# Input load order, modulation rows and HGRN head halves in a hybrid HGRN2 / mLSTM / PEER layer

## The chip, the cores and the metric

The kernel runs on one core of one Trainium2 chip. The metric is the device time of one execution in microseconds (us). A program that runs on the chip is compared by the median of several runs.

## The reference, cut to what matters

The layer takes 1024 latent tokens and 256 context tokens of width 1024. A conditioning vector gives six modulation vectors for the latent tokens and six for the context. Of these, the first two (shift and scale) are needed before anything else, the other four only behind the mixers.

```
mod_l = silu(c) @ w_mod + b_mod ; mod_c = silu(c_ctx) @ w_mod + b_mod
sh1, sc1, g1, sh2, sc2, g2 = split(mod, 6)            # for latent and for context tokens
p = (LN(tokens) * (1 + sc1) + sh1) @ w_in             # 9 blocks of 512 columns and 16 gate columns
o_hg = HGRN2 heads (4), forward and backward: S_t = diag(f_t) S_{t-1} + k_t v_t^T, o_t = S_t^T q_t,
       f = lb + (1 - lb) * sigmoid(z), k = 1 - f
h_ml = mLSTM heads (4), both directions, gates log_i = g_i, log_f = log_sigmoid(g_f)
x = LN(alpha * x + g1 * (readout @ w_out)) ; x = LN(alpha * x + g2 * PEER(LN(x) * (1 + sc2) + sh2))
```

PEER is a retrieval of 16 of 16384 single-neuron experts in each of 8 heads. It takes about two thirds of the time and is not touched.

## The kernel before, in words

Tokens lie in 10 tiles of 128: two of context, eight of x. Their modulated, transposed form xmT is kept as an f16 part and a bf16 remainder, so each projection is three matmul passes for each of 8 slices of the width.

**Prologue.** modcols (L84) loads two context tiles, then the first 2048 columns of w_mod in 8 row slices of 1 MB, and after half of these the weight block W(HI). Each slice feeds three matmuls of 2 x 512 (L116); the last 512 columns are done on VectorE as multiply-adds into macc (L120, L122). The eight x tiles are loaded after that. The sums are copied out (L126), and turned into columns by 16 matmuls with a ones vector and 12 transposes (L130, L132), which gives modc. inputs_ln (L164) takes the tiles in groups of 2, 4 and 4: statistics (L145, L147), normalisation (L170), transposes on TensorE (L176), scale and shift on ScalarE (L180), a cast to f16 on VectorE (L181), and the remainder on VectorE, or on GpSimd for every third slice (L182).

**Gates.** hgrn (L342) first calls gates (L237): 16 gate columns are projected for all tiles (into the bank oa), transposed to rows (L261), put through log-sigmoid as rows of 1280 (L266 to L270), scanned (L280 to L299), exponentiated, and transposed back into columns (L331), with a last small matmul group (L337). Then come modrows (L669), the values' projection inputs(0) and inputs(1) with 8 preparations of U behind each (uprep, L188), and the heads.

**modrows** computes the other four modulation vectors for the latent tokens: 32 tiles wm of 128 x 1024 in two buffers, for each of them two matmuls of 1 x 512 in quarters of the array, eight rows added to b_mod (L692) and stored to mrow (L693). mrow is read for g1 (L777) and for the mixing rows (L771), behind the mixers.

**Heads.** For each pair hh of heads the query weights are loaded and two heads projected (L500); then, for both directions d and both heads, one (L388) projects the forget gate (L222), takes sigmoid, logarithm and a scan (L394 to L404), builds the scaled keys and queries (L409 to L425), transposes keys (L431), and runs states, scores and outputs (L444 to L491). In it ten preparations of U are called: load of a 0.5 MB tile us (L195), cast on ScalarE (L198), remainder on GpSimd (L199), store (L202).

**Order.** The program is scheduled when it is built: each engine takes, by a modelled time line, what is ready and was written first; storage is given out in pools, and a tile that lies on an older tile's place waits for its readers. On the chip each engine then keeps that order. An instruction marked keep_in_program_order stays behind all that was written before it on its engine. All transfers here are issued by SP.

Of the kernel before, what the change touches and what calls it, by code (L numbers as in the profile page):

```python
# [6 lines left out]
F32 = mybir.dt.float32  # L7
# [81 lines left out]
def modcols(g, I, mp, lp):  # L89
# [16 lines left out]
    ps = [g.pp.tile([128, 512], F32, name=n, bufs=2 if n == "pj" else 1) for n in ("pj", "pj", "sc")]  # L106
# [17 lines left out]
    mr = mp.tile([128, 2048], F32, name="w0", bufs=8)[0:2]  # L124
    for b in range(3):
        (nc.scalar.copy if b % 2 else nc.vector.tensor_copy)(mr[:, b * 512:(b + 1) * 512], ps[b][0:2])  # L126
    pt = g.pp.tile([128, 512], F32, name="tr", bufs=2)
    for b in range(12, 16):
        for j in range(2):
            nc.tensor.matmul(pt[:, 2 * b + j:2 * b + j + 1], acc[:, j, (b - 12) * 128:(b - 11) * 128], g.ones, start=True, stop=True)  # L130
    for b in range(12):
        nc.tensor.transpose(pt[:, 2 * b:2 * b + 2], mr[:, b * 128:(b + 1) * 128], g.ident[0:2, 0:2])  # L132
    nc.vector.tensor_tensor(g.modc, pt[:, 0:32].rearrange("p (b j) -> p b j", j=2),
                            bT[:, :, None].to_broadcast([128, 16, 2]), op=OP.add)
# [29 lines left out]
def inputs_ln(g, xs, sp):  # L164

    nc = g.nc
    for t0, n in ((0, 2), (2, 4), (6, 4)):
# [4 lines left out]
        for k in range(KD):  # L172
# [8 lines left out]
            nc.vector.tensor_copy(g.xmT[0][:, k, sl], f)  # L181
# [55 lines left out]
def gates(g, I, w):  # L237
    nc, tc = g.nc, g.tc
    gp = g.gp
    with tc.tile_pool(name="gt", bufs=1, reuse_waits="tile") as tp:  # L240
        gb = tp.tile([128, 16], F32, name="gb")
# [1146 lines left out]
```

## Time and profile before

| what | value |
|---|---|
| median of 3 runs | 3186.1 us (3183.93 to 3199.63) |
| the profiled execution | 3201.39 us |
| its span | 3199.5 us, mean granted TensorE clock 0.952 |
| busy, share of the span | TensorE 91%, VectorE 80%, GpSimd 57%, ScalarE 37% |
| DMA | 900.31 MB, mean 281 GB/s |

The profile is of one execution, and its times count from the start of the span. The shares are averages over stages with different limits, so they say little about a change in the first 550 us: what such a change is worth is read from the stretches in which it acts and from what ends the waits there.

### The profile page before, as it was taken

To read this page: it belongs to the slowest core of one execution; us is meant where nothing else is said; L and a number is where in the kernel's file an instruction comes from. 1 tells how busy PE (TensorE), PEld (TensorE's weight loads), DVE (VectorE), ACT (ScalarE), POOL (GpSimd) and SP (SyncE) were. 2 spreads that over 40 slices of the span, in tenths; PEclk is the share of its full clock that TensorE was granted. 3 is DMA by queue.
4 is the path that set the end of the run, shared out by engine and by line. 5 is a ranking of instruction groups with operands and counts; after the bars stand their busy time and mean duration, and the time that the engine had idled before them with its cause. 6 is when DMAs were issued, how large, how long until landed. Compare 5 with 4: busy or idle time off the path is not lost.

```text
span 3199.5 us, 50493 instructions
## 1 busy us (share of the span) xinstructions
PE 2925.7 (91%) x18943; PEld 1890.1 (59%) x18943; DVE 2562.6 (80%) x5352; ACT 1180.8 (37%) x1699; POOL 1838.3 (57%) x1358
## 2 busy tenths in 40 slices
PE   7898999887898799899999999999999999999992
PEld 4644556556786566577778875555555555555541
DVE  8434464999878899798777777988888888888898
ACT  4464563325345432126666653222222222212211
POOL 3555675422347456416656666766666666666664
PEclk8999998998999899999999999999999999999996
DMA  7688666411267689767889999999999999999985
GB/s 282 212 290 290 214 207 238 145 60 60 100 214 268 225 297 333 276 232 261 294 283 312 316 345 338 371 347 350 364 363 362 363 341 368 362 357 364 358 306 190
DMA packets 319546, 900.31 MB, mean 281 GB/s; under 512 B 28077, under 2 KB 107573, under 8 KB 311365
## 3 DMA queue, kind: packets, MB, share of 16 engines
q1 hardware_dynamic: 208708, 494.38, 44.3%
q0 software_dynamic: 110592, 402.70, 33.6%
q8 instruction: 149, 2.44, 0.3%
q14 instruction: 97, 0.79, 0.1%
HBM read 758.67 MB, written 138.30 MB: 280 GB/s over the span
## 4 chain that ended last, share of the span: by engine, by line
PE 43%; DVE 26%; DMA 11%; issue 8%; POOL 6%; ACT 4%; SPq 0%; another core or an unknown queue 0%; DVEq 0%; POOLq 0%; ACTq 0%
PE y L1164 17%; PE S L1131 14%; DMA row<-in_peer_v_dram,idx 5%; DVE mz L555 3%; DVE row L1091 3%; PE pj L222 3%; PE y L1039 2%; DMA us<-in_peer_ut_dram 2%; DVE hg L1099 2%; POOL row L1072 2%; POOL uT L199 2%; PE pj L230 2%; DVE us L1034 1%; PE pj L833 1%; PE S L910 1%
## 5 line engine op out<-in xcount | busy, mean ns | idle before, releaser
L1131 PE MATMUL S<-hTd,uT 128*128 128x320 f16 (+1 forms) x6144 | 889.6, 301 | 15.6 <-ACT ge L1136 11.2
L1164 PE MATMUL y<-vs,w 128*128 128x512 bf16 x3840 | 857.3, 381 | 14.0 <-ACT vs L1146 6.8
L1131 PEld LDWEIGHTS <-uT 128*128 128x128 bf16 x6144 | 605.4, 99 | 270.8 <-issue 18.3
L1164 PEld LDWEIGHTS <-w 128*128 128x128 bf16 x3840 | 377.0, 98 | 452.3 <-issue 23.4
L1099 DVE SCALAR_TENSOR_TENSOR hg<-row,dot,hg 128x1024 f32<-128x1024 f32 x381 | 489.7, 1285 | 117.2 <-DMA row<-in_peer_v_dram,idx 107.8
L1072 POOL DMA_INDIRECT row<-in_peer_u_dram,idx x384 | 382.7, 997 | 288.2 <-DVE row L1091 144.6
L1072 POOL DMA_INDIRECT row<-in_peer_v_dram,idx x384 | 381.4, 993 | 215.2 <-DVE hg L1099 135.2
L1091 DVE SCALAR_TENSOR_TENSOR row<-row,hg 128x1024 f32<-128x1024 f32 x384 | 460.7, 1213 | 51.5 <-DMA row<-in_peer_u_dram,idx 48.5
L199 POOL TENSOR_TENSOR uT<-us,uT 128x1024 bf16<-128x1024 f32 x128 | 303.8, 2379 | 192.6 <-ACT uT L198 175.6
L1146 ACT CAST vs<-vf 128x1024 bf16<-128x1024 f32 x128 | 129.8, 1042 | 489.1 <-PE y L1164 255.4
L1147 POOL TENSOR_TENSOR vs<-vf,vs 128x1024 bf16<-128x1024 f32 x128 | 280.3, 2201 | 40.6 <-ACT vs L1146 37.4
L1035 POOL TENSOR_TENSOR kT<-us,gf 128x512 f32<-128x512 bf16 x160 | 177.3, 1135 | 193.8 <-DVE us L1034 158.1
L1136 ACT ACTIVATE ge<-S 128x320 f32<-128x320 f32 x256 | 112.6, 441 | 471.5 <-PE S L1131 377.7
L222 PE MATMUL pj<-xmT,wb 128*128 128x512 f16 (+3 forms) x1248 | 262.9, 367 | 19.3 <-ACT pad L545 17.6
L230 PE MATMUL pj<-wb,xmT 128*128 128x256 f16 (+1 forms) x1728 | 222.9, 289 | 25.2 <-DVE rsg L748 14.7
L1171 DVE TENSOR_TENSOR ya<-ya,y 128x512 f32<-128x512 f32 x310 | 210.1, 681 | 31.1 <-PE y L1164 29.6
L230 PEld LDWEIGHTS <-xmT 128*128 128x128 f16 (+1 forms) x1968 | 185.6, 103 | 67.6 <-issue 27.0
L222 PEld LDWEIGHTS <-wb 128*128 128x128 f16 (+1 forms) x1248 | 123.9, 101 | 147.4 <-issue 43.5
L1040 ACT COPY gst<-y 128x512 f32<-128x512 f32 x160 | 171.2, 1075 | 89.4 <-PE y L1039 69.6
L1034 DVE TENSOR_TENSOR us<-iob,eT 128x512 bf16<-128x512 bf16 x320 | 163.5, 559 | 25.5 <-ACT kT L1036 21.1
L198 ACT CAST uT<-us 128x1024 bf16<-128x1024 f32 x128 | 133.3, 1044 | 122.3 <-DMA us<-in_peer_ut_dram 101.5
L1039 PE MATMUL y<-kT 128*128 128x128 f32 x1280 | 161.5, 279 | 10.8 <-ACT kT L1036 9.8
(390 smaller groups left out, 3882.0 us busy)
## 6 DMA issues: line engine op xcount, KB each, us to landing
us<-in_peer_ut_dram SPq DMA_DIRECT2D x128, 512.0 KB
Ud<-uT SPq DMA_DIRECT2D x128, 512.0 KB
uT<-Ud SPq DMA_DIRECT2D x128, 512.0 KB
vf<-in_peer_v_dram SPq DMA_DIRECT2D x128, 512.0 KB
Gd<-gst SPq DMA_DIRECT2D x20, 1984.0 KB
Gt<-Gd SPq DMA_DIRECT2D x31, 1280.0 KB
Sd<-ge SPq DMA_DIRECT2D x66, 320.0 KB
kT<-Sd SPq DMA_DIRECT2D x66, 320.0 KB
```

Of the source, the lines that this page charges most:

```text
L199: nc.gpsimd.tensor_tensor(lo, uf, hi, op=OP.subtract)
L222: g.nc.tensor.matmul(ps[:, :t1 - t0], w.t[a][:, k, c0:c0 + 128], g.xmT[b][:, k, t0:t1], start=(k == 0 and a == b), stop=(k == KD - 1 and a ...
L230: g.nc.tensor.matmul(ps, g.xmT[a][:, k, t * 128:(t + 1) * 128], w.t[b][:, k, :w.n], start=(k == 0 and a == b), stop=(k == KD - 1 and a == 1))
L1034: nc.vector.tensor_tensor(cm[:, a], g.iob, eT[:, a, None, t0:t0 + 4].to_broadcast([128, 128, 4]), op=OP.is_equal)
L1039: nc.tensor.matmul(ps[:, i * 128:(i + 1) * 128], oh[:, 0, i], oh[:, 1, i], start=True, stop=True)
L1072: d = g.nc.gpsimd.indirect_dma_start(out=b, out_offset=None, in_=self.I["peer_u" if n < 128 else "peer_v"][0], in_offset=bass.IndirectOffs ...
L1091: nc.vector.scalar_tensor_tensor(b, b, 1.0, self.ps, op0=OP.mult, op1=OP.mult, accum_out=dot[:, j:j + 1])
L1099: nc.vector.scalar_tensor_tensor(self.ps, b, dot[:, j:j + 1], self.ps, op0=OP.mult, op1=OP.add)
L1131: m = nc.tensor.matmul(ps[:, :hn], uT[:, a, k, :], g.hTd[b][:, k, i * hn:(i + 1) * hn], start=(k == 0 and (a, b) == (0, 0)), stop=(k == KD ...
L1147: nc.gpsimd.tensor_tensor(v[:, 1], vf, v[:, 0], op=OP.subtract)
L1164: nc.tensor.matmul(ps, w[:, a, t * 128:(t + 1) * 128], v[:, b, h * 512:(h + 1) * 512], start=(n == 0), stop=(n == 3 * GI - 1))
L1171: nc.vector.tensor_add(ya, ya, ps)
```

## The change

The prologue loads both context tiles and the first four x tiles ahead of w_mod, and the other four x tiles and W(HI) behind it. All 2048 columns of w_mod are computed on TensorE, in four matmuls per slice that lie in the four quarters of the array, into one bank; the multiply-adds on VectorE, the ones matmuls and 12 of the transposes go, four full transposes come. In inputs_ln every odd slice's cast to f16 is made by ScalarE from PSUM instead of by VectorE.

gates takes the log-sigmoid on the small column tiles before the transposes, uses two banks for these, and returns its last part, cols, which hgrn calls behind inputs(1) and its 8 preparations; the first tile's transposes in it are pinned to program order. The gates' pool is closed there, and the heads' pools lie in its place.

modrows is cut into two calls, one for each half, which stand between front and one of the last two head passes (hh = 1, d = 1). Its pool is opened ahead of the gates' pool.

one is cut into front (projection, sigmoid, logarithm, scan) and one (the rest). In each pair the forward front of the first head stands ahead of the query projection, and that of the second head between the two heads' query projections.

```diff
-    acc = mp.tile([128, 2, 512], F32, name="macc")
-    xs = inputs_load(g, I, lp, 0, 2)
+    xs = inputs_load(g, I, lp, 0, 6)
     for k in range(KD):
-        if k == KD // 2:
-            g.w0.append(W(g, I, HI))
...
-        for b in range(3):
-            nc.tensor.matmul(ps[b][0:2], g.cs[:, k::8], wt[:, b * 512:(b + 1) * 512], start=(k == 0), stop=(k == KD - 1))
-        for j in range(2):
-            c = g.cs[:, 8 * j + k:8 * j + k + 1]
-            if k == 0:
-                nc.vector.tensor_scalar(acc[:, j], wt[:, 1536:], c, None, op0=OP.mult)
-            else:
-                nc.vector.scalar_tensor_tensor(acc[:, j], wt[:, 1536:], c, acc[:, j], op0=OP.mult, op1=OP.add)
-    xs += inputs_load(g, I, lp, 2, NT)
+        for q in range(4):
+            nc.tensor.matmul(ps[32 * q:32 * q + 2], g.cs[:, k::8], wt[:, q * 512:(q + 1) * 512], start=(k == 0), stop=(k == KD - 1))
+    xs += inputs_load(g, I, lp, 6, NT)
+    g.w0.append(W(g, I, HI))
+    for q in range(4):
+        o = slice(32 * q, 32 * q + 2)
+        (nc.scalar.copy if q % 2 else nc.vector.tensor_copy)(mr[o], ps[o])
...
+    for b in range(4):
+        nc.tensor.transpose(pt[:, b * 128:(b + 1) * 128], mr[:, b * 128:(b + 1) * 128], g.ident)
...
-            nc.vector.tensor_copy(g.xmT[0][:, k, sl], f)
+            if k % 2:
+                nc.scalar.activation(g.xmT[0][:, k, sl], pt[:, :n * 128], AF.Identity, scale=g.modc[:, 8 + k, j:j + 1], bias=g.modc[:, k, j:j + 1])
+            else:
+                nc.vector.tensor_copy(g.xmT[0][:, k, sl], f)
...
-def gates(g, I, w):
+def gates(g, I, w, tp):
...
+    nc.vector.tensor_tensor(f, psv[:, :, 1], gbv[:, None, 1].to_broadcast([128, NT, 2, 4]), op=OP.add)
+    nc.scalar.activation(e, f, AF.Abs)
+    nc.scalar.activation(e, e, AF.Exp, scale=-1.0)
+    nc.scalar.activation(e, e, AF.Ln, bias=1.0)
...
+            pt = g.pp.tile([128, 512], F32, name=("sc", "up")[t0 // 4 % 2])
...
-        nc.scalar.activation(e, fr, AF.Abs)
-        nc.scalar.activation(e, e, AF.Exp, scale=-1.0)
-        nc.scalar.activation(e, e, AF.Ln, bias=1.0)
-        lf = fr
-        nc.vector.scalar_tensor_tensor(lf, fr, 0.0, e, op0=OP.min, op1=OP.subtract)
...
+    def cols():
         g.col = gp.tile([128, NT, 3, 2, 4], F32, name="gcol")
...
-                nc.tensor.transpose(pt[:, i * 64:(i + 1) * 64], s[:, t, :], g.ident[0:64, 0:64])
+                mm = nc.tensor.transpose(pt[:, i * 64:(i + 1) * 64], s[:, t, :], g.ident[0:64, 0:64])
+                if t == 0:
+                    tc.keep_in_program_order(mm)
...
+    return cols
...
-        gates(g, I, w1)
-        modrows(g, I, es.enter_context(tc.tile_pool(name="mr", bufs=1, reuse_waits="tile")))
+        mr = es.enter_context(tc.tile_pool(name="mr", bufs=1, reuse_waits="tile"))
+        gs = es.enter_context(ExitStack())
+        cols = gates(g, I, w1, gs.enter_context(tc.tile_pool(name="gt", bufs=1, reuse_waits="tile")))
...
         inputs(1)
         g.uprep(8)
+        cols()
+        gs.close()
...
-        def one(hd, d, w, q):
+        def front(hd, d, w):
...
+            return bF, b, kr, last, ref
+
+        def one(hd, d, q, bF, b, kr, last, ref):
...
-            w = W(g, I, HQ + 256 * hh)
+            w = W(g, I, HF0 + 256 * hh)
+            f = [front(2 * hh, 0, w)]
+            wq = W(g, I, HQ + 256 * hh)
...
-            for d in range(2):
-                w = W(g, I, (HF0, HF1)[d] + 256 * hh)
-                for e in range(2):
-                    one(2 * hh + e, d, w, qs[e])
+                if e == 0:
+                    f.append(front(2 * hh + 1, 0, w))
+            for e in range(2):
+                one(2 * hh + e, 0, qs[e], *f[e])
+            w = W(g, I, HF1 + 256 * hh)
+            for e in range(2):
+                f = front(2 * hh + e, 1, w)
+                if hh:
+                    modrows(g, I, mr, e)
+                one(2 * hh + e, 1, qs[e], *f)
...
-def modrows(g, I, mp):
+def modrows(g, I, mp, h):
```

## Rows read from the trace of the kernel before

**Rows 1.** Table of stretches: busy us (instructions) per engine, granted clock, DMA share, GB/s.
```profile
0.00:31.50 31.50, 22.26 (x51) 4.46 (x52) 20.16 (x42) 5.24 (x6) 4.50 (x6) 1.00 0.92 371
31.50:82.40 50.90, 37.90 (x369) 28.73 (x368) 50.75 (x91) 27.33 (x46) 28.10 (x16) 0.73 0.64 227
82.40:146.60 64.20, 52.55 (x487) 45.00 (x488) 35.49 (x42) 28.62 (x37) 33.57 (x12) 0.89 0.60 205
146.60:211.00 64.40, 61.37 (x314) 27.35 (x311) 13.82 (x9) 33.36 (x45) 37.64 (x16) 0.97 0.73 264
211.00:331.00 120.00, 108.81 (x599) 52.99 (x599) 58.74 (x74) 67.57 (x78) 72.30 (x32) 0.96 0.86 295
...
431.00:534.00 103.00, 93.64 (x582) 66.43 (x581) 57.95 (x95) 47.94 (x62) 65.63 (x30) 0.83 0.60 204
534.00:777.00 243.00, 203.49 (x1358) 144.00 (x1358) 210.10 (x418) 88.60 (x119) 84.10 (x34) 0.92 0.32 108
```
The engine columns are TensorE matmul, weight load, VectorE, ScalarE, GpSimd.

**Rows 2.** Chain of waits, 0 to 300 us: start, length, what.
```profile
10.00 19.94 DMA w<-in_w_mod_dram
30.04 1.42 DVE macc L122 x2
```

**Rows 3.** Groups of instructions by form, 31.5 to 82.4 us: busy us, mean ns.
```profile
L181 DVE CAST xmT<-xf 128x512 f16<-128x512 f32 x16 | 10.5, 683 | 0.0
L145 DVE BATCH_NORM_STATS2 lnst<-xt 128x6 f32<-128x512 f32 x16 | 10.1, 665 | 0.0
L170 DVE TENSOR_SCALAR xt<-xt,lnmv,lnrs 128x1024 f32<-128x1024 f32 x8 | 8.3, 1043 | 0.0
...
L180 ACT ACTIVATE xf<-tr,modc 128x512 f32<-128x512 f32 x8 | 6.1, 777 | 5.7 <-DVE xmT L182 4.6 <-POOL xmT L182 1.1
```

**Rows 4.** Timeline of TensorE, 80 to 170 us: start, length, what, [idle before, releaser].
```profile
105.70 14.57 PE L230 MATMUL pj<-wb,xmT 128*128 128x256 f16 x132
125.39 0.34 PE L331 MATMUL sc<-ident,row 64*128 64x64 f32 x1 [5.11 <-DVE row L284]
...
141.79 0.36 PE L331 MATMUL sc<-ident,ge 64*128 64x64 f32 x1 [6.53 <-ACT ge L320]
...
142.20 4.57 PE L230 MATMUL pj<-wb,xmT 128*128 128x256 f16 x24
```

**Rows 5.** Timeline of VectorE, 82 to 147 us.
```profile
105.90 0.42 DVE L262 COPY row<-sc 64x256 f32<-64x256 f32 x1 [2.48 <-PE sc L261]
...
116.25 2.81 DVE L280 TENSOR_TENSOR_SCAN ga<-one,row 32x1280 f32<-32x1280 f32 x1
...
141.11 1.48 DVE L325 TENSOR_TENSOR ga<-ga,gM 64x1280 f32<-64x1280 f32 x1
```

**Rows 6.** Timeline of ScalarE, 80 to 170 us.
```profile
84.35 1.90 ACT L76 CAST wb<-wf 128x2048 f16<-128x2048 f32 x1 [4.67 <-PE oa L230]
...
111.84 1.28 ACT L268 ACT_TABLE_LOAD   x1
113.13 1.27 ACT L268 ACTIVATE ge<-ge 64x1280 f32<-64x1280 f32 x1
```

**Rows 7.** Waits, 160 to 545 us: who waited for whom, us in total, times, longest.
```profile
PE sc L471 <- DVE qt L424: 8.6, 5, 2.7
...
PE tr L431 <- DVE kh L422: 5.4, 3, 4.0
```

**Rows 8.** Groups of instructions, 160 to 545 us: busy us, mean ns, idle before.
```profile
L686 PE MATMUL tr<-wm,cs 128*1 128x512 f32 x128 | 33.5, 618 | 8.3 <-DMA wm<-in_w_mod_dram 8.3
```

**Rows 9.** Timeline of SP's DMA issues, 0 to 50 us.
```profile
31.23 1.60 SPq L195 DMA_DIRECT2D us<-in_peer_ut_dram  x2
```

**Rows 10.** Waits, 211 to 331 us.
```profile
ACT uT L198 <- DMA us<-in_peer_ut_dram: 18.7, 10, 3.6
```

**Rows 11.** Waits, 431 to 534 us.
```profile
ACT uT L198 <- DMA us<-in_peer_ut_dram: 13.0, 6, 7.0
```

**Rows 12.** Timeline of VectorE, 550 to 556 us.
```profile
554.26 0.75 DVE L553 TENSOR_SCALAR mz<-pad,cwT 128x1024 f32<-128x1024 f32 x1 [23.13 <-ACT pad L545]
```

More of the change, by code (lines that the diff above doesn't have):

```diff
@@ L123, in modcols @@
-    xs += inputs_load(g, I, lp, 2, NT)
-    mr = mp.tile([128, 2048], F32, name="w0", bufs=8)[0:2]
-    for b in range(3):
-        (nc.scalar.copy if b % 2 else nc.vector.tensor_copy)(mr[:, b * 512:(b + 1) * 512], ps[b][0:2])
-    pt = g.pp.tile([128, 512], F32, name="tr", bufs=2)
[L128 to L132, printed above, removed]
@@ new lines, in gates @@
+    gb = tp.tile([128, 16], F32, name="gb")
+    nc.sync.dma_start(gb, rowb(I["ml_gate_b"], 0, 16))
+    ps = g.pp.tile([128, 512], F32, name="oa")
+    for t in range(NT):
+        proj_t(g, w, t, ps[:, t * 16:(t + 1) * 16])
+    gt = tp.tile([128, NT, 2, 64], F32, name="gt")
+    nc.vector.memset(gt, 0.0)
+    psv = ps[:, :NT * 16].rearrange("p (t a d h) -> p t a d h", a=2, d=2, h=4)
+    gbv = gb.rearrange("p (a d h) -> p a d h", a=2, d=2)
+    f = tp.tile([128, NT, 2, 4], F32, name="gf")
+    e = tp.tile([128, NT, 2, 4], F32, name="gl")
@@ new lines, in gates @@
+    rows = []
+    for a in range(2):
+        r = tp.tile([64, SQ], F32, name=f"row{a}")
+        for t0 in range(0, NT, 4):
+            n = min(4, NT - t0)
+            pt = g.pp.tile([128, 512], F32, name=("sc", "up")[t0 // 4 % 2])
+            for i in range(n):
+                nc.tensor.transpose(pt[0:64, i * 128:(i + 1) * 128], gt[:, t0 + i, a, :], g.ident)
+            nc.vector.tensor_copy(r[:, t0 * 128:(t0 + n) * 128], pt[0:64, :n * 128])
+        rows.append(r)
+    ir, fr = rows
+    e = tp.tile([64, SQ], F32, name="ge")
@@ new lines, in gates @@
+    lf = fr
+    one = tp.tile([64, NT, 128], F32, name="one")
+    neg = tp.tile([64, NT, 128], F32, name="neg")
+    nc.vector.memset(one, 1.0)
+    nc.vector.memset(neg, 0.0)
+    nc.vector.memset(one[:, :, 0:1], 0.0)
+    nc.vector.memset(neg[:, :, 0:1], -BIG)
+    oneF, negF = (x.rearrange("p t s -> p (t s)") for x in (one, neg))
+    a = tp.tile([64, NT, 128], F32, name="ga")
+    aF = a.rearrange("p t s -> p (t s)")
+    nc.vector.tensor_tensor_scan(aF[0:32], oneF[0:32], lf[0:32], 0.0, op0=OP.mult, op1=OP.add)
@@ new lines, in gates @@
+    mpb = mp_[:, :, None].to_broadcast([64, NT, 128])
+    nc.vector.tensor_tensor(M, M, mpb, op=OP.max)
+    negM = tp.tile([64, LAT], F32, name="negM")
+    nc.vector.tensor_scalar(negM, MF[:, CTX:], -1.0, None, op0=OP.mult)
+    nc.sync.dma_start(g.negM, negM)
+    win = tp.tile([64, LAT], F32, name="win")
+    wv = fr.rearrange("p (t s) -> p t s", s=128)
+    nc.vector.tensor_tensor(wv, mpb, M, op=OP.subtract)
+    nc.scalar.activation(win, wv.rearrange("p t s -> p (t s)")[:, CTX:], AF.Exp)
@@ L327, in gates @@
+    nc.sync.dma_start(g.win, win)
+    ws = e.rearrange("p (t s) -> p t s", s=128)
+    nc.vector.tensor_tensor(ws, gq, ml[:, :, None].to_broadcast([64, NT, 128]), op=OP.subtract)
+    nc.scalar.activation(ws, ws, AF.Exp)
+    cd = tp.tile([64, NT], F32, name="gcd")
+    nc.vector.tensor_sub(cd, mp_, ml)
+    nc.scalar.activation(cd, cd, AF.Exp)
+    fl = a
+    nc.vector.tensor_add(fl, a, M)
+    nc.scalar.activation(fl, fl, AF.Exp, scale=-1.0)
+    def cols():
         g.col = gp.tile([128, NT, 3, 2, 4], F32, name="gcol")
```

165 lines of the change are left out of this document (58 added, 107 removed).

## The prediction

> **What bounds the kernel now.** I read the table of stretches first. The reader should look at it as five regimes [rows 1]. Up to 31.5 us the DMA engines are 92% busy at 371 GB/s and the first third of w_mod's columns is awaited. From 31.5 to 82.4 us VectorE is busy 50.75 of 50.90 us: layer norm and modulation, one engine saturated while ScalarE has 23 us free. From 82.4 to 146.6 us TensorE should be the bound (gate columns, then both halves of the HGRN input projection), yet it is busy 52.55 of 64.20 us. [...] From 534 us on the mLSTM convolution has VectorE busy 210 of 243 us. Everything behind that (mixing, expert stage) has the same instructions in both versions, so I take it to start earlier or later as a block.
>
> Then I asked what ends the waits: in the prologue the last w_mod tile lands at about 30.0 us [rows 2]; in the gate stretch TensorE stands still twice, 5.11 us for a VectorE scan result and 6.53 us for a ScalarE exponential [rows 4]; in the heads the named waits are short [rows 7, 8].
>
> The sum is made against the profiled execution, 3201.4 us (span 3199.5 and 1.9 around it). It lies 15.3 us over the median of 3186.1; I subtract the same microseconds from both. The three runs shown differ by 15.7 us among themselves, so 0.5% (16 us) is about what a measurement can tell from no change.
>
> **Prologue.** Ahead of the last w_mod tile the queue now holds 6 input tiles and 8 MB of weights instead of 2 input tiles, W(HI) and 8 MB: 1.05 MB more, at 371 GB/s 2.8 us later, so about 32.8 us. The multiply-add on VectorE that ended the old wait (1.42 us [rows 2]) is gone, replaced by four small matmuls of about 1 us (records of the same width in the modulation rows take 618 ns, two side by side [rows 8]). The stretch thus starts 2.4 us later (32.8 + 1.1 against 31.5). Removed from VectorE behind it: norm of four tiles, which now fits into the DMA wait (VectorE is busy 20.2 of 31.5 us there even with the multiply-adds). 16 statistics took 10.1 us and 8 normalisations 8.3 us for 8 tiles [rows 3], so 2.30 us a tile, 9.2 us. Half of the casts go to ScalarE: 8 wide ones at 683 ns are 5.5 us (the four narrow ones I leave out). VectorE alone would finish at 82.4 + 2.4 - 14.7 = 70.1 us. ScalarE gains 8 activations of 777 ns (6.2 us [rows 3]) and the cast of W(HI) (like the one of 1.90 us [rows 6]), which moves from the DMA wait to here: 27.3 + 8.1 = 35.4 us of work, nearly all behind the modulation columns at about 38 us, so 73.5 us if packed. I take 71.4, a gain of **11**; the ends are 12.3 (VectorE alone) and 3, if ScalarE keeps 6 us of gaps. W(HI) now lands near 42 us instead of 20; its cover is the modulation, as TensorE is busy only 37.9 of the 50.9 us there.
>
> **Gates.** The softplus is now taken on small column tiles before the transposes, and what ends in column form (cols) stands behind inputs(1). The two idle times, 5.11 and 6.53 us, go if the chain is ready before inputs(1) ends. The old chain's core runs from 116.25 to 142.59 us [rows 5], 26.3 us, and 1.3 us for the last exponential. Before it lie about 7 us for the gate columns, three tiny activations and two table loads of 1.28 us, and six rounds of transposes, now in two banks instead of one. The last row copy came at 105.90 [rows 5], 21.6 us behind the gate projections' end at about 84.3 (there the waiting cast began [rows 6]); some 18 of that were transposes, and I put 9 to 18 us for them. So 44 to 53 us behind the gate projections. TensorE's own work there is 146.6 - 84.3 - 11.6 = 51 us less what the clock gives back: 24 matmuls took 4.57 us after the second idle, 190 ns each, against 110 ns before [rows 4], so 1.9 us. That is 49 us, and the chain is late by 4 us at worst. VectorE's work is unchanged, so if cols is late, the first front's key tile (it lies in the gates' storage) and the head behind it wait. Gain between 8.5 and 13.5; I take **12**.
>
> Each table load in the trace is followed at once by its activation: 1.28 us from 111.84, next start 113.13 [rows 6]. [...]
>
> **Fronts.** Projection, sigmoid, logarithm and scan of a head pair's first heads now run beside the query projections. TensorE's waits on what follows them, 8.6 us for qt and 5.4 us for kh [rows 7], are spread over eight head passes, and two of these get a new order: 2/8 of 14 is 3.5. Ends 0 and 14; I take **4**. Late next is the state recurrence, which is not touched.
>
> **Modulation rows.** Moved are 32 loads of 0.5 MB, 8 short loads, 8 stores and 128 matmul records; all 48 transfers are on SP's queue, past the remaining weight loads and the loads (tile us) and stores of U's preparation. Their result is read far behind the heads. What leaves the early heads is 33.5 us of TensorE busy and 8.3 us of waits for wm [rows 8], where TensorE is 91 to 95% busy. In the last heads, 431 to 534 us, TensorE has 9.4 us idle and 17.5 us lost to the half clock ((1 - 0.83) of 103 us). If all of this can be filled, 41.8 go and 14.9 come: a gain of 27. If instead the DMA engines decide, 16.8 MB at the 295 GB/s of the wm stretch are 57 us, 40% of 103 us are free, and the 16 us that don't fit come on top of the same matmuls and waits: a loss of 16. Both ends are resources that the rows show half used; I take the middle, a gain of **5**.
>
> **Sum:** 11 + 12 + 4 + 5 = 32 us. 3201.4 becomes 3169.4, the median 3186.1 becomes **3154.1**. All upper ends together are 67 us, all lower ones a loss of 4.
>
> **Rivals.** *The rows float.* The place of a call is only a rank: U's first load goes out at 31.23 us [rows 9], though its call stands behind inputs(0). The rows' storage now lies ahead of the gates' and is free from the prologue's end, so their matmuls may fill gaps from 80 us on, much as now. Then that part is worth 0: 11 + 12 + 4 = 27, 3159 us. Against it: the loads are lowest in rank until the heads before them are placed. Chance 0.13.
>
> *ScalarE takes over.* The prologue ends at 79 us, cols is late and the fronts bring nothing: 3 + 8.5 = 11.5, 3174.6 us. For it: ScalarE's 73.5 us is already above VectorE's 70.1. Against it: seven of its casts are U's and can wait. Chance 0.18.
>
> *U's loads stand behind the rows' loads (slower).* ScalarE takes its work in order, and its cast of U waits for the tile us, with the exponentials of the head queued behind it and TensorE behind these. Ten preparations are called per head pass, 20 in the two. If each of their loads stands behind two wm tiles, 1.05 MB at 295 GB/s, it comes 3.6 us later: 72 us, and with the other parts' 27 the time is 3231. The change is slower as soon as the mean delay passes 27/20 = 1.35 us. Against it: ScalarE waited 18.7 us for that tile in the 120 us with wm loads [rows 10] and 13.0 us in the 103 us without [rows 11], 16% against 13% of the time, only 3 us for such a stretch. Chance 0.12. [...]
>
> **How the numbers follow.** The forecast has 0.57. Faster by over 0.5% is the forecast and the floating rows, 0.70; within 0.5% is ScalarE's case, 0.18; slower is 0.12. The range leaves out the slower case and the outermost ends: 3122 (64 us) to 3188 (a loss of 2).
>
> **What would show it.** Right: modulation ends near 71 us, with VectorE and ScalarE both near full; no TensorE wait over 3 us at the gate scan or exponential, inputs(1) done near 124 us; the wm records lie between 380 and 520 us with waits under 10 us; the first convolution step comes some 30 us before 554.3 [rows 12]. Wrong: wm records from 80 us on (floating), ScalarE without gaps up to 79 us, waits for the tile us that double in the last heads, or a convolution that starts earlier while the end does not.

## The result, and the profile after

The change is slower: 3212.7 us median (3206.7 to 3234.7, 8 runs) beside 3187.9 of the kernel before (8 runs); the ratio is 1.0088, interval 1.0069 to 1.0106. 3154.1 was forecast.

The table of stretches of the changed kernel, to be held against [rows 1], with one more stretch, 501 to 551 us (columns as there):

```profile
0.00:31.50 31.50, 14.04 (x63) 1.95 (x63) 14.71 (x45) 4.52 (x9) 0.90 (x6) 0.97 0.92 373
31.50:82.40 50.90, 34.21 (x367) 26.86 (x364) 43.36 (x59) 34.96 (x56) 26.12 (x16) 0.65 0.63 223
82.40:146.60 64.20, 47.67 (x454) 41.60 (x451) 40.02 (x43) 23.49 (x35) 31.79 (x11) 0.89 0.57 198
431.00:534.00 103.00, 69.93 (x351) 31.20 (x351) 34.14 (x66) 29.75 (x34) 52.74 (x26) 0.79 0.87 306
501.00:551.00 50.00, 15.86 (x41) 1.19 (x42) 5.97 (x15) 12.85 (x14) 22.33 (x12) 0.63 0.94 336
534.00:777.00 243.00, 204.78 (x1341) 141.01 (x1338) 180.97 (x341) 81.50 (x111) 70.55 (x30) 0.91 0.31 101
```

VectorE is relieved in the prologue, but TensorE does less in the gate stretch than before (47.67 against 52.55 us), and from 501 to 551 us it works 15.86 of 50 us. The group of the rows' matmuls, those that compute the moved modulation rows (160 to 545 us, against [rows 8]):

```profile
L702 PE MATMUL tr<-wm,cs 128*1 128x512 f32 x128 | 40.2, 793 | 35.4 <-DMA wm<-in_w_mod_dram 35.4
```

The list of waits of 31.5 to 545 us has two rows for wm tiles, one for TensorE's weight loads and one for its matmuls. First the kernel before, then the changed one:

```profile
PEld tr L686 <- DMA wm<-in_w_mod_dram: 11.2, 5, 4.9
PE tr L686 <- DMA wm<-in_w_mod_dram: 8.3, 5, 4.0
```

```profile
PEld tr L702 <- DMA wm<-in_w_mod_dram: 50.0, 13, 8.4
PE tr L702 <- DMA wm<-in_w_mod_dram: 35.4, 8, 6.7
```

The weight load and the matmul of a tile wait for the same load at the same time; here the same gap on both, in the changed kernel:

```profile
523.65 0.09 PEld L702 LDWEIGHTS tr<-wm,cs 128*1 128x1 f32 x4 [8.45 <-DMA wm<-in_w_mod_dram]
```

```profile
523.65 3.14 PE L702 MATMUL tr<-wm,cs 128*1 128x512 f32 x8 [6.67 <-DMA wm<-in_w_mod_dram]
```

So the two rows don't add up to idle time: the matmuls stood still for 35.4 us, where it was 8.3. The expectations below add them (85 us for the changed kernel), and their bounds are meant that way.

The same list of 431 to 534 us, against [rows 11]: ScalarE's wait for the tile us trebles.

```profile
ACT uT L193 <- DMA us<-in_peer_ut_dram: 38.7, 11, 10.7
```

VectorE's first convolution step, 32 us later than in [rows 12]; by the ratio the whole is 28 us longer. (The profiled execution of the kernel before took longer than any of its 8 timed runs, so the ends of the two profiles lie only 6.5 us apart.)

```profile
586.04 0.75 DVE L570 TENSOR_SCALAR mz<-pad,cwT 128x1024 f32<-128x1024 f32 x1 [13.83 <-ACT pad L562]
```

TensorE's timeline behind the last head:

```profile
504.14 3.16 PE L702 MATMUL tr<-wm,cs 128*1 128x512 f32 x8 [3.97 <-DMA wm<-in_w_mod_dram]
...
533.28 3.17 PE L702 MATMUL tr<-wm,cs 128*1 128x512 f32 x8 [6.49 <-DMA wm<-in_w_mod_dram]
542.39 2.95 PE L702 MATMUL tr<-wm,cs 128*1 128x512 f32 x8 [5.94 <-DMA wm<-in_w_mod_dram]
551.22 4.95 PE L225 MATMUL pj<-wb,xmT 128*128 128x256 f16 x26 [5.88 <-ACT mv L537]
```

A pair of tiles comes every 10 us, and almost nothing else runs. The values' projection of the mLSTM stage (L225), which ran from 518 us in the kernel before, starts only at 551.22, and its last releaser is ScalarE's copy of the first values into mv (L537). That row proved to be the clue.

The way there, in us of each profiled execution (first and last head output, first convolution step), with every kernel that was run; each ratio is against runs of the kernel before on the same chip:

| kernel | ratio (95%) | median us | first head | last head | convolution |
|---|---|---|---|---|---|
| before | 1 | 3187.9 | 269.0 | 520.5 | 554.3 |
| changed | 1.0088 (1.0069–1.0106) | 3212.7 | 233.7 | 500.2 | 586.0 |
| rows_back | 0.9951 (0.9937–0.9966) | 3181.9 | 245.9 | 495.1 | 528.1 |
| rows_only | 1.0106 (1.0079–1.0133) | 3231.8 | 246.9 | 517.6 | 598.3 |
| cols_pinned | 1.0092 (1.0060–1.0124) | 3224.5 | 234.7 | 501.9 | 589.2 |
| no_prep_tail | 1.0161 (1.0136–1.0186) | 3249.4 | 232.5 | 491.5 | 560.8 |
| wm3 | 1.0056 (1.0034–1.0077) | 3204.4 | 230.4 | 494.5 | 559.5 |
| rows_mlstm | 1.0054 (1.0033–1.0076) | 3204.9 | 232.8 | 495.0 | 528.7 |
| mr_last | 0.9965 (0.9947–0.9983) | 3176.6 | 233.7 | 512.1 | 548.4 |
| prologue_only | 1.0004 (0.9991–1.0017) | 3188.9 | 267.2 | 522.8 | 555.1 |
| fronts_only | 1.0018 (1.0005–1.0032) | 3194.3 | 271.7 | 516.1 | 550.1 |
| gates_only | 0.9987 (0.9971–1.0003) | 3187.5 | 261.2 | 517.6 | 549.9 |
| gates_fronts | 0.9950 (0.9931–0.9970) | 3169.5 | 247.8 | 500.7 | 531.9 |
| prologue_gates | 0.9997 (0.9982–1.0012) | 3187.1 | 258.0 | 514.1 | 547.3 |
| late_exp | 0.9951 (0.9936–0.9966) | 3168.0 | 247.6 | 499.2 | 531.1 |
| late_both | 0.9900 (0.9884–0.9916) | 3153.5 | 232.5 | 485.2 | 516.6 |
| late_both_nou | 0.9928 (0.9913–0.9944) | 3163.8 | 234.3 | 487.9 | 521.9 |
| mr_last_fix | 1.0054 (1.0037–1.0071) | 3202.4 | 237.7 | 510.8 | 548.3 |

The kernel before took 3196.9 us in the set of the first four experiments, 3186 to 3189 in the others; so medians of different sets are not compared here.

### The profile page after: what moved, and what is told of

It is laid out like the page before. It is cut to its first block, busy times and chain, and to the rows that moved or that the text cites. A ratio compares the mean times of both kernels' runs of the same rounds, so it can differ in the third digit from the quotient of the medians.

```text
span 3206.0 us, 50480 instructions
## 1 busy us (share of the span) xinstructions
PE 2897.1 (90%) x18935; PEld 1873.6 (58%) x18935; DVE 2545.6 (79%) x5324; ACT 1192.7 (37%) x1718; POOL 1831.1 (57%) x1359
## 4 chain that ended last, share of the span: by engine, by line
PE 39%; DVE 17%; DMA 8%; issue 3%; POOL 3%; ACT 1%; SPq 0%; DVEq 0%; ACTq 0%; POOLq 0%
PE y L1180 22%; PE S L1147 14%; DMA row<-in_peer_v_dram,idx 4%; DVE row L1107 4%; DVE hg L1115 2%; PE y L1055 2%; DVE us L1050 2%; DMA row<-in_peer_u_dram,idx 1%; DMA us<-in_peer_ut_dram 1%; DVE alt L894 1%; POOL kT L1051 1%; DMA Gd<-gst 1%; DVE w L1168 1%; DVE ind L896 1%; PE pj L849 1%
## 5 line engine op out<-in xcount | busy, mean ns | idle before, releaser
L217 PE MATMUL pj<-xmT,wb 128*128 128x512 f16 (+3 forms) x1248 | 261.2, 363 | 8.4 <-ACT pad L562 8.1
L225 PE MATMUL pj<-wb,xmT 128*128 128x256 f16 (+1 forms) x1728 | 222.1, 288 | 33.4 <-DVE rsg L764 14.6
L225 PEld LDWEIGHTS <-xmT 128*128 128x128 f16 (+1 forms) x1968 | 186.1, 103 | 74.6 <-issue 36.4
```

The costliest lines, as they stand in the source:

```text
L217: g.nc.tensor.matmul(ps[:, :t1 - t0], w.t[a][:, k, c0:c0 + 128], g.xmT[b][:, k, t0:t1], start=(k == 0 and a == b), stop=(k == KD - 1 and a ...
L225: g.nc.tensor.matmul(ps, g.xmT[a][:, k, t * 128:(t + 1) * 128], w.t[b][:, k, :w.n], start=(k == 0 and a == b), stop=(k == KD - 1 and a == 1))
```

## Experiments

**Where the loss is: rows_back.** The two calls go back behind the gates.

```diff
+        modrows(g, I, mr, 0)
+        modrows(g, I, mr, 1)
...
-                if hh:
-                    modrows(g, I, mr, e)
```

> The changed kernel with both calls of modrows put back behind gates; prologue, cols and fronts stay changed. Theory (tail): the changed kernel loses because its last ten w_mod tiles of the modulation rows come at the pace of the DMA engines once the heads are done, about 45 us from 501 to 546 us in which TensorE does nothing else, with the values' projection (26 us, done among the heads before) queued behind. Put back, the time should fall from 3213 to 3165 to 3195, not slower than before. Rival (gates): the loss is the 13.1 us wait at the hoisted second tile of cols and a prologue that gained nothing; then this kernel stays slower than before, 3200 or more.

0.9951: the place of the rows costs 1.0088 - 0.9951 = 0.0137, or 44 us, and what is left of the change gains 16.

**rows_only:** the kernel before with that move alone.

```diff
-        modrows(g, I, es.enter_context(tc.tile_pool(name="mr", bufs=1, reuse_waits="tile")))
...
+                    if hh and d:
+                        modrows(g, I, mr, e)
```

> The kernel before with nothing but modrows moved between the last head passes (its pool opened ahead of the gates' pool). Tail theory: slower than before by 10 to 40 us, with waits of TensorE for wm of 60 us or more behind the last head. Gates rival: the same as before within 10 us, or faster, as the early heads lose 41.8 us of TensorE time.

1.0106, and the convolution starts 44 us late, though the first head output comes 22 us earlier. The move loses by itself.

**Is it the shared DMA queue? no_prep_tail** leaves U's 20 preparations out of the last two head passes; they are made later, in the mixing.

```diff
+            up = (lambda m: None) if hd > 1 and d else g.uprep
...
-                        g.uprep(1)
+                        up(1)
```

> The changed kernel without the 20 preparations of U in the last two head passes; the same 20 are made later, in the mixing stage, so nothing is left out. If the tail is the DMA engines' sharing between U's 40 transfers and the 32 wm tiles, the waits for wm fall from 85 us to under 40 and the first convolution step comes by 20 us or more earlier; the mixing stage may give some of it back. If it is the latency of two buffers alone, the waits fall by less than 20 us.

TensorE's waits for wm fell to 17.4 us for the matmuls and 33.5 for the weight loads, in sum between the two bounds of the expectation, and the convolution came 25 us earlier. So U's transfers are part of these waits. But the stages behind paid more than that: from the read of g1 to the end it took 2400.1 us against 2341.7 in the changed kernel, and TensorE was busy 5.75 of 60 us at 1100 to 1160 us (53.83 in the changed kernel). With U's casts away from ScalarE's queue, the list of waits in 440 to 600 us shows what the copy into mv waits for:

```profile
ACT mv L539 <- DMA mrow<-bb: 21.3, 1, 21.3
```

**wm3:** three buffers for wm.

```diff
-            wt = mp.tile([128, 1024], F32, name="wm", bufs=2)
+            wt = mp.tile([128, 1024], F32, name="wm", bufs=3)
```

> The changed kernel with three buffers for the tiles of w_mod instead of two, nothing else. If the rows among the last heads wait for the bandwidth that they share with U (DMA share 0.94 at 501 to 551 us), a third buffer brings little: TensorE's waits for wm stay over 60 us of the 85, and the ratio to the kernel before stays at 1.004 to 1.010. If they wait for the latency of a load that starts only when a buffer comes free, the waits fall to about half (40 us) and the time falls by 20 to 35 us: ratio 0.998 to 1.003.

Half of the expectation held: the matmuls' waits for wm went from 35.4 to 10.3 us (with the weight loads' from 85.4 to 26.3), so much of them was time from issue to landing that two buffers didn't cover. But the time fell by only 0.0032 (10 us, and the two intervals overlap) and not by 20 to 35 us, and the stretch 501 to 551 us still stood at 31.45 us of TensorE, until ScalarE's copies into mv came at 521.30, behind the rows' stores at 514.33 to 517.29. So waiting for wm is not what most of the loss consists of.

**rows_mlstm** moves the rows into the mLSTM stage (wm in U's two load buffers, bb in a pool of its own).

```diff
-                if hh:
-                    modrows(g, I, mr, e)
...
                 one(2 * hh + e, qk[e], qk[2 + e])
+                if hh == 0:
+                    modrows(g, I, mr, e)
```

> The changed kernel with the modulation rows moved on into the first head pair of the matrix memory stage (LSTM), their tiles taken from U's two buffers for loads. My theory: the place among the last heads is bad because there the loads share the queue with two U loads and two U stores in each 10 us, and because the values' projection stands behind the rows in TensorE's order; in a stage where the DMA engines are busy for some 0.2 to 0.3 of the time the loads cost no wait. TensorE's waits for wm fall from 85 us to under 25, the last head output comes near 455 to 465 us (500 less the 42 us of the rows), and the time is that of the kernel with the rows put back: ratio 0.995 (0.991 to 1.000) to the kernel before. Rival: the rows cost the same wherever they stand late, since U's preparations follow them there and take buffers from them: waits over 50 us and a ratio of 1.004 or more.

The waits for wm stayed under 25 us, as expected (6.7 and 8.6), but the ratio is 1.0054, over my bound. From the convolution to the read of g1 it takes 328.2 us, 294.7 with rows_back: 33.5 us more, as much as the 128 row matmuls are busy. TensorE is idle for 49 us of that stage, and for 53 with rows_back: there was idle time, but the rows came on top of it. Why they didn't fill it wasn't tried. And the heads end no earlier, though they began 13 us ahead and have 33 us less to do. Two rows of the same stretch, first rows_mlstm, then rows_back:

```profile
431.00:501.00 70.00, 64.62 (x291) 46.22 (x292) 30.42 (x62) 21.42 (x27) 34.43 (x17) 0.54 0.51 169
```

```profile
431.00:501.00 70.00, 64.67 (x398) 46.19 (x396) 38.82 (x71) 29.87 (x36) 45.17 (x21) 0.80 0.63 219
```

The same busy time, at a granted clock of 0.54 and 0.80: 291 matmuls against 398. The mix isn't quite the same, but in the trace of the kernel before, one and the same matmul (oa<-S,qe, median) took 298 ns at a clock of 1.00 (498 to 501 us) and 447 ns at 0.50 (515.5 to 518 us). What lowers the clock wasn't tried, and this is one execution of each.

**The storage: mr_last.** The kernels with the rows among the last heads have one thing in common. In the changed kernel the first write to mv, on VectorE, waits for the rows' stores out of bb (mrow<-bb); the second row is the same instruction in mr_last:

```profile
549.82 0.09 DVE L530 MEMSET mv<- 128x40 f32 x1 [1.58 <-DMA mrow<-bb]
```

```profile
509.31 0.09 DVE L530 MEMSET mv<- 128x40 f32 x1
```

So mv lies where bb lay. The wait is short in the trace because the order was fixed when the program was built: the values' copies and, behind two full banks, their matmuls were placed behind the stores. mr_last moves one line, so that the rows' pool lies behind those of the heads:

```diff
-        mr = es.enter_context(tc.tile_pool(name="mr", bufs=1, reuse_waits="tile"))
         gs = es.enter_context(ExitStack())
...
         sp = es.enter_context(tc.tile_pool(name="hs", bufs=5, reuse_waits="tile"))
+        mr = es.enter_context(tc.tile_pool(name="mr", bufs=1, reuse_waits="tile"))
```

> The changed kernel with one line moved: the pool of the rows' tiles (wm, bb) is opened behind the heads' pools instead of ahead of the gates', nothing else. In the changed kernel the first write to the values' storage of the next stage (mv) waits for the rows' four stores: mv takes the place of bb. Theory of the storage: TensorE's 50 idle microseconds at 501 to 551 us are there because the values' two banks can't be copied out before the rows are stored; with mv elsewhere the values' projection goes on from about 505 us, fills TensorE between the pairs of wm tiles, the first convolution step comes at 545 to 565 us instead of 586, and the ratio to the kernel before falls from 1.009 to 1.002 or less (0.996 to 1.003), though TensorE still waits for wm. Rival: TensorE's order, in which the values stand behind the rows, and U's loads on the same queue hold it up; then the convolution stays at 575 to 590 us and the ratio at 1.006 to 1.011.

0.9965: the changed kernel becomes faster than the one before. The stretch behind the last head:

```profile
501.00:551.00 50.00, 49.90 (x321) 28.78 (x321) 12.60 (x25) 15.40 (x23) 21.04 (x9) 0.97 0.89 303
```

and ScalarE's first copies into mv, 41 us earlier:

```profile
509.24 0.65 ACT L537 COPY mv<-pj 128x256 f32<-128x256 f32 x2 [3.80 <-PE oa L491]
```

TensorE is full, with the DMA engines 0.89 busy; the rows' matmuls run on to 564.2, now among the values', and wait 6.1 us for wm. Of the 0.0137 that the place of the rows cost, 0.0123 (39 us) goes with this one line. The fall of the waits for wm is in it: they shrink because TensorE has other work between the pairs.

**The parts alone: prologue_only, fronts_only, gates_only,** each in the kernel before, with the functions of the change and nothing else.

```diff
 # prologue_only: modcols, inputs_ln
 # gates_only
+        cols = gates(g, I, w1, gs.enter_context(tc.tile_pool(name="gt", bufs=1, reuse_waits="tile")))
+        modrows(g, I, mr)
 # fronts_only
+            f = [front(2 * hh, 0, w)]
```

> The kernel before with the changed prologue alone (order of the loads, w_mod in quarters of the array, half of the casts as activations); gates, rows and heads as before. My prediction priced this part at 11 us (3 to 12). From the trace of the changed kernel, where the gate projections end only 0.8 us earlier, I now expect 0 to 3 us: ratio 0.999 to 1.001, the gate projections ending at 83 to 84.5 us. Rival: the gain is there, and only the other parts hide it in the changed kernel: ratio under 0.998, the gate projections ending under 80 us.

> The kernel before with the heads in two parts alone (the forward gate projection of the pair ahead of the queries); prologue, gates and rows as before. The prediction priced this part at 4 us (0 to 14). With the prologue alone at 1.0004 and the rows put back at 0.9951, gates and fronts together are worth some 15 us. Of the lead of that kernel over the one before, 23 of 25 us are there at the first head output, ahead of most of the heads' work, so I expect the larger share from the gates: this part alone 0.999 (0.9975 to 1.0005). Rival: the heads are what gained, with 0.996 or less here, and the gates gave next to nothing.

> The kernel before with the gates of the changed kernel alone (logarithms taken ahead of the transposes, transposes through two banks, gate columns after the second input projection); prologue, rows and heads as before. The prediction priced this part at 12 us (8.5 to 13.5). By the runs so far, if the parts add, it is the difference of the kernel with the rows put back (0.9951) and the other two parts alone (1.0004 and 1.0018), that is 0.993 or 23 us. My theory: this part alone gives 0.993 (0.9915 to 0.9945); TensorE's waits at the gate columns' transposes (5.0 us on VectorE, 5.5 us on ScalarE) go, a wait of some 10 us on ScalarE's copies comes, and the gain is that the rows' matmuls start up to 70 us earlier, in the shadow of the gates' chain, without the waits for w_mod that they have at 170 to 320 us in the kernel before. Rival: the parts don't add; the gates alone give the priced 12 us or less (0.996 or above) and the rest of the 15 us needs the heads or the prologue with them.

1.0004, as expected; 1.0018, a little above its range; 0.9987, the rival's side. Each is under the noise bound of 0.5%, and together they don't make 0.9951: the parts don't add. Two pairs told which belong together (the functions as above):

```diff
 # gates_fronts: gates and heads of the change
 # prologue_gates: modcols, inputs_ln and gates of the change
```

> The kernel before with the changed gates and the heads in two parts; prologue and rows as before. The three parts of the kernel with the rows put back (0.9951) don't add: alone they give 1.0004 (prologue), 1.0018 (heads) and 0.9987 (gates). My theory: gates and heads need each other. The gates let the rows run early, and only the new order of the heads fills TensorE behind them (72 to 78 us busy of each 80 us at 325 to 485 us, against 65 to 73 us with the gates alone); then this kernel gives 0.995 (0.9935 to 0.9965), and the prologue adds nothing here either. Rival: the prologue is needed too, and this gives 0.998 or more.

> The kernel before with the changed prologue and the changed gates; heads and rows as before. By the theory that gates and heads need each other this gives no more than the gates alone: 0.9985 (0.997 to 1.0005). Rival: the prologue, by which the input projection starts ahead of the gates, is what the gates need: 0.996 or less.

0.9950 and 0.9997: the gain is that of gates and heads together, 16 us, and the prologue adds nothing. With the gates alone TensorE is busy 138.3 us of 325 to 485 us, with both 147.9; that much the stretches show, a single wait that explains it they don't.

**TensorE's wait in the gates: cols_pinned.** In the changed kernel TensorE and ScalarE stand still in the gate stretch:

```profile
127.67 0.36 PE L330 MATMUL up<-ident,ge 64*128 64x64 f32 x1 [13.06 <-ACT ge L317]
```

```profile
126.34 1.27 ACT L317 ACTIVATE ge<-ge 64x1280 f32<-64x1280 f32 x1 [14.59 <-DVE ge L316]
127.52 0.20 ACT L320 ACTIVATE gcd<-gcd 64x10 f32<-64x10 f32 x1
127.62 1.03 ACT L193 CAST uT<-us 128x1024 bf16<-128x1024 f32 x1
128.55 0.36 ACT L382 COPY hv<-pj 128x256 f32<-128x256 f32 x1
```

Only the first tile of cols is pinned; the second stands ahead of the input projection on TensorE. cols_pinned pins all.

```diff
-                if t == 0:
-                    tc.keep_in_program_order(mm)
+                tc.keep_in_program_order(mm)
```

> The changed kernel with every transpose of cols pinned to program order, not the first tile's alone. Gates theory: the 13.1 us wait goes, inputs(1) ends near 136 us instead of 149, and the time falls by 8 to 13 us. Tail theory: the heads come 10 us earlier, but the end of the modulation rows' loads is set by the DMA engines; the time falls by 0 to 8 us and stays above before.

No gain: the wait is now 14.66 us on the copy into hv, by which ScalarE frees the banks of the projection. The rows above show why: the copy (128.55) stands behind the exponential (126.34), which waited 14.59 us for VectorE, and ScalarE took them in that order.

**late_exp** issues the four late exponentials behind the seventh copy of inputs(1) (rows behind the gates, all of cols pinned).

```diff
+                m = nc.scalar.copy(v[:, t, 256 * b:256 * b + 256], ps[:, :256])
+                if b:
+                    tc.keep_in_program_order(m)
+                if b and t == 6:
+                    late()
```

> The changed kernel with the modulation rows put back behind the gates, all transposes of the gate columns kept in the order of the program, and the four late exponentials of the gates (decays, win, ws, floors) issued behind the seventh copy of the second input projection instead of ahead of it. My theory: the wait of TensorE in the second input projection is ScalarE's queue: an exponential that waits for VectorE's chain stands ahead of the copies that free the two projection banks. With the exponentials behind those copies the wait of about 10 us at 120 to 130 us goes, the second input projection ends about 9 us earlier, and the ratio to the kernel before goes from 0.995 (rows put back alone) to 0.992 (0.990 to 0.993), some 3165 to 3175 us where the kernel before takes 3197. Rival: the wait only moves on, to the copies of the gate columns or to the first gate projections of the heads; then the milestones from 165 us on stand where they stood and the ratio stays at 0.995 (0.9935 to 0.9965).

No change against rows_back, as the rival had it: the wait on ScalarE was gone, and another had come. TensorE, and SP's issues:

```profile
136.20 1.87 PE L709 MATMUL tr<-wm,cs 128*1 128x512 f32 x4 [11.24 <-DMA wm<-in_w_mod_dram]
```

```profile
109.40 0.92 SPq L706 DMA_DIRECT2D wm<-in_w_mod_dram  x2
127.82 0.50 SPq L309 DMA_DIRECT2D negM<-negM  x1
```

SP issues nothing for 17 us: the store of negM, at the end of VectorE's chain, stands ahead of the loads, and the DMA share falls to 0.26 there. The changed kernel has the same gap (109.42 to 127.02), the kernel before a shorter one (127.68 to 139.81).

**late_both** also makes negM on ScalarE, behind the exponentials, so that its store comes later in SP's queue.

```diff
-    nc.vector.tensor_scalar(negM, MF[:, CTX:], -1.0, None, op0=OP.mult)
-    nc.sync.dma_start(g.negM, negM)
...
+        keep(negM, MF[:, CTX:], AF.Identity, scale=-1.0)
+        nc.sync.dma_start(g.negM, negM)
```

> The kernel with the late exponentials and, besides, the negated running maximum made by ScalarE behind them instead of by VectorE ahead of them, so that its store (negM) and that of win no longer stand in SyncE's queue ahead of the loads of w_mod and U. Seen so far: with the exponentials moved, TensorE's wait on ScalarE went, and 11.2 us of waiting for a w_mod tile took its place, while SyncE issued nothing from 110.3 to 127.8 us, standing at the store of negM, and the DMA engines stood idle. My theory: two queues that keep their order, ScalarE's and SyncE's, hold up TensorE there, and either alone gains nothing. With both freed TensorE waits under 4 us in all from 100 to 165 us, the first head output comes some 10 us earlier than the 246 us of the kernel with the rows put back, and the ratio to the kernel before is 0.991 (0.9885 to 0.9935). Rival: the stage is held by the DMA engines' bytes or by the heads behind it, and the ratio stays at 0.995 (0.994 to 0.9965).

0.9900: some 32 us under the kernel before, and 16 under late_exp. SP's queue alone, with the exponentials left where they were, wasn't tried. The stretch of the gap, first late_exp, then late_both:

```profile
110.40:127.80 17.40, 14.56 (x122) 10.92 (x120) 17.15 (x17) 4.33 (x8) 12.11 (x3) 0.98 0.26 92
```

```profile
110.40:127.80 17.40, 17.40 (x145) 12.77 (x143) 17.14 (x16) 4.88 (x9) 12.10 (x3) 1.00 0.83 272
```

**late_both_nou** holds U's first preparations back to the end of the prologue.

```diff
+            if t0 == 6 and k == KD - 1:
+                g.tc.keep_in_program_order(m)
...
+        g.uprep(8, pin=True)
         inputs(0)
```

> The same with U's first preparations held back until the last activation of the inputs' normalisation. My theory of the prologue: VectorE's casts and remainders, 0.3 to 0.7 us each, take 2.0 to 2.5 us (one normalisation 4.3 us) whenever GpSimd makes a remainder of U or of a weight, some nine times from 43 to 78 us, and so the order of the loads gains nothing. Without U's six remainders there VectorE's busy time from 31.5 to 82 us falls from 43 us to 32 to 36 us, the gate projections end 3 to 8 us earlier than the 83.5 us of the changed kernel, and the time is 2 to 7 us under that of the kernel with both queues freed. Rival: ScalarE, with half of the casts, sets the pace there (35 us busy), and the gate projections end at 82 to 84 us as before; or they end earlier and U's preparations, late by 40 us, cost it again, with a ratio equal to or above that of the kernel with both queues freed.

Half of it came. VectorE's casts, first in late_both, then here (31.5 to 82 us; busy us, mean ns):

```profile
L176 DVE CAST xmT<-xf 128x512 f16<-128x512 f32 x8 | 7.3, 906 | 1.9 <-ACT xf L172 1.9
```

```profile
L178 DVE CAST xmT<-xf 128x512 f16<-128x512 f32 x8 | 4.3, 534 | 3.1 <-ACT xf L172 3.0
```

The gate projections end at 75.4 us instead of 82.6, but the first head output comes 2 us later and the ratio is 0.9928, as the second half of the rival had it: the preparations, put off, are most likely paid behind it. (VectorE's busy time fell to 37.59 us, not quite to my 32 to 36.)

**mr_last_fix:** the changed kernel with both findings, mr_last and the queues of late_both.

```diff
+        mr = es.enter_context(tc.tile_pool(name="mr", bufs=1, reuse_waits="tile"))
...
+        keep(negM, MF[:, CTX:], AF.Identity, scale=-1.0)
```

> The same with the gates' late exponentials and stores moved as in the kernel with both queues freed: the change as it was meant, rows among the last heads, with what the runs found mended. With the rows behind the gates both queues freed gave 0.990, 0.005 less than without. Theory of the storage: the same step comes here, 0.991 to 0.998. Rival: 1.001 or more, since rows among the last heads have no work beside them. I expect it to stay above the 0.990 of the rows behind the gates, where their loads share DMA engines that wait for nothing else.

1.0054, the rival's side, though not for its reason: TensorE is busy 49.77 us of 501 to 551 us. But the edit didn't free TensorE in the gate stretch here. TensorE, then ScalarE, of mr_last_fix:

```profile
138.74 4.30 PE L225 MATMUL pj<-wb,xmT 128*128 128x256 f16 x24 [9.69 <-ACT hv L384]
```

```profile
133.07 1.06 ACT L314 ACTIVATE win<-row 64x1024 f32<-64x1024 f32 x1 [5.62 <-DVE row L317]
```

Without the rows' matmuls between them the first seven copies of inputs(1) are done at 126.2 us, and the exponentials behind them still wait for VectorE's chain, with the next copies and TensorE behind them. In late_both the seventh copy comes at 132.7, the exponentials follow without a wait, and TensorE waits for none of them. So the first head output comes at 237.7, 4 us later than in mr_last. That isn't all: the last head output and the convolution come no later than in mr_last, and g1 is read 14 us later (846.3 against 832.1). What makes up the 0.0089 (28 us) between the two kernels is left open.

## Why the prediction was wrong

**Modulation rows: the step that failed.** It weighed two resources, TensorE's free time (+27) and the DMA engines (-16), and took +5 (the half clock in the first is in the trace of the kernel before: granted 1.00 at 491 to 501 us, 0.50 at 505 to 518 us); the place of the rows measured -44. What it left out stands in its own sentence that the result "is read far behind the heads": it asked who reads the result, and not who gets the storage. The first tile of the next stage takes the rows' place and may not be written before the rows are stored; so the values' projection, which used to run among the last heads, stood behind them. Without that wait the place measures 0.9965 - 0.9951, a loss of 4 us, which the intervals of the two ratios don't tell from nothing: within the step's bounds. That they would run late and not float was right (all matmuls, and all loads but two, come at 390 us or later), and so was the early lead: the first head output came 35 us ahead. In the terms of the sum the runs give 0 for the prologue, 16 for gates and fronts together and -44 for the rows, a loss of 28 us where a gain of 32 was forecast.

**Prologue: 11 forecast, 0 measured.** The load order did what was said (w_mod's last matmuls ended at 34.2 us, 33.9 was said), but the modulation ended at 80.4 us and not 71. VectorE's busy time fell by 7.4 us, not 14.7, and it was idle for 7.5 us of the stretch: 2.1 at the start, for which the step had 2.4, and 3.7 waiting for ScalarE's slices, for which its sum of VectorE's work had nothing. The start itself had changed: VectorE waited for the x tiles that now lie behind w_mod, and took its copies of the w_mod sums between their statistics.

```profile
33.59 1.28 DVE L137 BATCH_NORM_STATS2 lnst<-xt 128x6 f32<-128x512 f32 x2 [15.40 <-DMA xt<-in_x_dram]
```

So the modulation columns were ready at 42.0 us (37.8 before, about 38 in the step), and ScalarE, which cast W(HI) first, scaled its first slice at 43.24 (38.03 before). The choice of 71.4 was also below the step's own packed 73.5 for ScalarE.

For the busy time the step took means from [rows 3] and multiplied them by fewer instructions. Those means contain waits: in the rows below, instructions that met a remainder on GpSimd took longer and ended about when that ended. VectorE, then GpSimd, of the changed kernel:

```profile
41.18 0.77 DVE L162 TENSOR_SCALAR xt<-xt,lnmv,lnrs 128x1024 f32<-128x1024 f32 x1
...
43.45 4.27 DVE L162 TENSOR_SCALAR xt<-xt,lnmv,lnrs 128x1024 f32<-128x1024 f32 x1
47.64 0.28 DVE L176 CAST xmT<-xf 128x256 f16<-128x256 f32 x1
...
49.97 2.23 DVE L177 TENSOR_TENSOR xmT<-xf,xmT 128x256 bf16<-128x256 f32 x1
52.12 2.21 DVE L176 CAST xmT<-xf 128x256 f16<-128x256 f32 x1
```

```profile
43.10 4.06 POOL L77 TENSOR_TENSOR wb<-wf,wb 128x2048 bf16<-128x2048 f32 x1 [41.56 <-ACT wb L76]
...
49.74 4.43 POOL L194 TENSOR_TENSOR uT<-us,uT 128x1024 bf16<-128x1024 f32 x2
```

A normalisation of 0.77 us took 4.27, a cast of 0.28 took 2.21; each of the three long ones ended within 0.6 us of GpSimd's instruction (47.2; 54.2; and for the one in between some 52.0, an estimate, halfway through the last row, which holds two). In these rows the waits go with GpSimd's work and not with the number of VectorE's instructions, and that work hardly shrank (26.1 us from 28.1): W(HI)'s remainder came into this stretch out of the DMA wait. So half the casts, at 907 ns instead of 683, cost 7.3 us and not 5.5. late_both_nou points the same way: with GpSimd busy 17.2 us there instead of 26.5 in late_both, its casts took 534 ns instead of 906. By what VectorE is held beside GpSimd's work no run shows. Whether an earlier end of the prologue would have paid isn't shown: in late_both_nou 7 us at its end were gone by the first head, but U's preparations had been put off there.

**Gates and fronts: 12 and 4 forecast, 16 measured together,** but 4 for the gates alone and a loss of 6 for the fronts: each of these under the noise bound of 0.5%. That the sum agrees is luck: the waits that the gates' step meant to remove aren't what was gained. The wait of 5.11 us went; the one of 6.53 us became 13.06, and inputs(1) ended at 148.9 us, not near 124 (146.8 before). The step asked whether the chain is ready before inputs(1) ends (VectorE's last operand is ready at 129.8: yes), but not what stands behind the waiting exponential and the waiting store. With both out of the way, late_both gained another 0.005, 16 us. (The step's lower end of 8.5 doesn't follow from its terms either: 13.5 less 4 is 9.5.)

**The rivals.** The slower case had 0.12, and its outcome came. Its mechanism, ScalarE waiting for the tile us, grew as it said (38.7 of 103 us, from 13.0, more than the doubling that was named as a sign), but it wasn't the main cause: in mr_last ScalarE still waits 24.2 us for that tile in the same stretch, and TensorE is full behind it. The floating rows didn't come. ScalarE did not take over: the prologue ended where that rival had it (80.4 us, 79 said), but ScalarE was idle for 16 us of the stretch.

## What to carry to other kernels

When a step is moved, look up whose place its tiles take and who takes theirs: in pools that reuse storage the next tenant waits for the last reader, and a late store can hold up a whole stage; one moved line was worth 39 us here. Before a mean duration is used as a price, look what ran beside it. Ahead of an instruction that waits on a long chain, look at each queue that keeps its order (here ScalarE's and SP's at once): freeing ScalarE's alone showed nothing, freeing SP's as well gave 16 us, and in mr_last_fix, with no other work in between, the same edit left TensorE a wait of 9.69 us. Price the parts of a change in pairs as well: gates and heads gave 16 us together and next to nothing alone.

## What the runs showed of the hardware

VectorE beside GpSimd's remainders, in the prologue of the changed kernel: a normalisation that took 0.77 us elsewhere took 4.27, and three casts that took 0.28 to 0.43 us elsewhere took 2.08 to 2.48; so a mean duration from that stretch was no price per instruction. TensorE's weight load and matmul waited for one load at the same time (8.45 and 6.67 us before 523.65), so their waits (50.0 and 35.4 us) don't add. Two loads of 0.5 MB, issued from 516.69 us on as their buffers came free, were followed by their matmuls at 523.65, some 7 us later, with the DMA engines 0.94 busy at 501 to 551 us; a third buffer cut the matmuls' waits for such loads from 35.4 to 10.3 us. With almost the same busy time in 70 us (64.62 and 64.67 us) TensorE made 291 matmuls at a granted clock of 0.54 and 398 at 0.80, in a mix that isn't quite the same; the matmul oa<-S,qe took 298 ns at 1.00 and 447 ns at 0.50.
